# Two products of the identity with itself ahead of each block's and each chain chunk's own products

## The chip, the cores and the metric

The kernel runs on one core of a Trainium2 chip. The metric is the device time of one execution in microseconds (us). Five engines matter here: PE (TensorE, matrix products; PEld are its weight loads), DVE (VectorE), ACT (ScalarE), POOL (GpSimd), and SP, which issues most transfers. TensorE's clock has two levels, 2.4 GHz and 1.2 GHz; the profile shows the granted one as 1.00 and 0.50.

## The reference

Two layers of a network over 512 latent and 256 context positions of width 1024. Each layer is a feed-forward part, a token mixing and a second feed-forward part. The mixing projects the input once, runs a windowed attention over four pairs of heads, and on the other half of the width a recurrence in both directions of time:

```python
px = nx @ w_in
attn_x = neighbourhood_attention(q_x, k_x, v_x, k_s, v_s, na_bias)
def step(S, inp):                       # 8 heads, two directions
    removal = jnp.einsum('bhvk,bhk->bhv', S, kk_t)
    S = S * w_t - removal[..., None] * (kk_t * a_t) + v_t[..., None] * k_t
    out = jnp.einsum('bhvk,bhk->bhv', S, r_t)
...
y_x = jnp.concatenate([attn_x, rwkv_x], axis=-1) @ w_out
```

Layer 0 also carries the context stream through the mixing's output; layer 1 does not.

## The kernel before

Activations lie with the width on the 128 partitions and the 768 positions along the free axis. The feed-forward parts stream weights and multiply in split float32. The change sits in the token mixing, `mix`.

`mix` runs several generators side by side through `drive` (line 74): `chains` (rank 0), `solves` (rank 1), `all_blocks` (rank 2), and, all at rank 3, `projections`, the modulation products of the coming parts (`fillers`), `attentions` and `outs` (the output projection). `drive` steps them by a model time; each step's instructions get a priority from the rank, and the framework's scheduler then orders every engine's instructions by readiness and priority. So the order on PE is not written out by hand: it is one in-order queue that the scheduler fills from all streams.

The recurrence is computed in chunks of 32 positions, in two groups of two head pairs, 24 chunks a group:

- `rwkv_block` (line 811) prepares, for one pair `p` and one half `u` of 128 positions, the operands (DVE, POOL and ACT), and at line 884 takes a PSUM bank `gt` from the tag `p` for each of the two directions and runs eight products of 64 rows by 64 columns into it (line 887). ACT and DVE copy the result into the stage tile `st`. There are 24 blocks and 48 such banks in a layer. `free_stage` holds back all but the first four blocks of a layer until `qkv_done[NP - 1]`, that is, until the projections are done.
- `rwkv_solve` and `rwkv_solves` invert the chunk's triangular systems: DVE work, then small products into `py`, `px` (lines 928, 936) and `ap` (line 790). These banks are also of the tag `p`, which has two banks in all; `lz` (line 828) and `bops` (line 745) use it too.
- `rwkv_chain` (line 945) carries the state from chunk to chunk. Line 969 takes the bank `ch`; the tag `ch` has one bank. Eight products (line 972) read the state `x`, ACT and DVE copy half of the bank back into `x`, eight products (line 978) fill the other half, and ACT and DVE copy that into `x2`, the next chunk's `x`. There are 48 chunks in a layer.

A product of float32 operands is two MATMUL instructions with a weight load each. `self.c(C_ID)` is a 128 by 128 identity that lies in SBUF from the start.

Of the kernel before, what the change touches and what calls it, by code (L numbers as in the profile page):

```python
# [29 lines left out]
H, HD, NP = 8, 64, 4  # L30
# [5 lines left out]
C_ID, C_MEAN, C_B64, C_J, C_MG, C_RST, C_BO2, C_EPS = (  # L36
    0, 128, 130, 258, 386, 450, 706, 708)
# [12 lines left out]
def rev(ap):  # L50
    a = [list(x) for x in ap.ap]
    s, n = a[-1]
    return bass.AP(tensor=ap.tensor, offset=ap.offset + s * (n - 1), ap=a[:-1] + [[-s, n]])


def free_ap(ap, dims, offset=0):
    return bass.AP(tensor=ap.tensor, offset=ap.offset + offset, ap=[list(ap.ap[0])] + [list(d) for d in dims])
# [52 lines left out]
class Net:  # L110
# [700 lines left out]
    def rwkv_block(self, l, p, b, emit, ltd, g):  # L811

        nc = self.nc
        y = p % 2
        ts = g["ts"][y]
        ins = [g["in"][y, n] for n in (b, (0, 2, 1)[b])]
        r, k, kk = [[t[:, n] for t in ins] for n in range(3)]
        lora = self.wp.tile([128, 2, 128], F32, name="lora", bufs=2)
        nc.sync.dma_start(out=lora, in_=self.a["lora"][l, :, :, 128 * p:128 * p + 128])
        spans = [self.span(b, d) for d in range(2)]  # L820
        order = lambda t, d: rev(t) if d else t

        th, tan = self.t("sp", "th", 512), self.t("sp", "tan", 512)
        for i, t in enumerate((th, tan)):
            rows = HALVES[i]
            ps = self.bank("p", "lz", (128, 2, 256))
            for d in range(2):
                nc.tensor.matmul(ps[:, d], lhsT=lora[rows, d], rhs=self.zin[rows, spans[d]], start=True, stop=True)
            for d in range(2):
                n = 8 * i + 4 * d + p  # L830
                self.act(t[:, 256 * d:256 * d + 256], order(ps[:, d], d), AF.Tanh, scale=0.5 - i, bias=self.rv[:, n:n + 1])
        if b == 0:
            self.tt(ts[:, spans[0]], tan[:, 0:256], rev(tan[:, 256:512]), ALU.add)
        else:
            for d in range(2):
                src = order(tan[:, 256 * d:256 * d + 256], d)
                if b == 1:
                    nc.gpsimd.tensor_scalar(ts[:, spans[d]], src, 1.0, None, ALU.mult)
                else:
                    self.tt(ts[:, spans[d]], ts[:, spans[d]], src, ALU.add)  # L840
        nc.vector.tensor_scalar(th, th, 1.0, None, ALU.add)
        for d in range(2):
            cs = slice(256 * d, 256 * d + 256)
            nc.vector.tensor_tensor_scan(out=th[:, cs], data0=self.c(C_RST, 256), data1=th[:, cs], initial=0.0, op0=ALU.mult, op1=ALU.add)
        pd = self.t("sp", "pd", 520).rearrange("p (s t) -> p s t", t=65)
        nc.gpsimd.memset(pd[:, :, 0:1], 1.0)
        self.act(pd[:, :, 1:65], th.rearrange("p (s t) -> p s t", t=64), AF.Exp, scale=-0.5 * DC)
        self.act(th, th, AF.Exp, scale=0.5 * DC, bias=self.eps(1))
        bks = []
        for d in range(2):  # L850
            kd, kkd = order(k[d], d), order(kk[d], d)
            c8 = lambda t: t.rearrange("p (c t) -> p c t", c=8)
            bk = self.t("sp", "bk", 512).rearrange("p (c a t) -> p c a t", c=8, a=2)
            ka, be = bk[:, :, 0], bk[:, :, 1]
            td = c8(tan[:, 256 * d:256 * d + 256])
            self.stt(be, td, -1.0, c8(kkd), ALU.add, ALU.mult)
            nc.gpsimd.tensor_scalar(ka, td, self.rv[:, 24 + p:25 + p], self.rv[:, 16 + p:17 + p], ALU.mult, ALU.add)
            self.tt(ka, ka, c8(kd), ALU.mult)
            self.tt(bk, bk, free_ap(th[:, 256 * d:256 * d + 1], [[32, 8], [0, 2], [1, 32]]), ALU.mult)
            bks.append(bk)  # L860
        for h in range(2):
            u = 2 * b + h
            yield from self.until(lambda: self.free_stage(p, u))
            st = self.t("st", "st", SW)
            g["stage"][y, u] = st
            c4 = lambda t: t.rearrange("p (s h t) -> p s h t", s=2, h=2)
            for e, rows in enumerate(SR):

                o = 1024 * e
                one = self.consts[rows, C_ID + 64 * e:C_ID + 64 * e + 64]  # L870
                nc.vector.tensor_scalar(free_ap(st[rows], [[256, 4], [1, 64]], o), free_ap(one, [[0, 4], [1, 64]]), 1.0, None, ALU.mult)
                self.tt(free_ap(st[rows], [[512, 2], [256, 2], [1, 64]], o + 128), free_ap(one, [[0, 2], [0, 2], [1, 64]]),
                        free_ap(pd[rows, 2 * h:2 * h + 1, 64], [[260, 2], [65, 2], [0, 64]]), ALU.mult, nc.gpsimd)
                if not emit:
                    nc.gpsimd.memset(free_ap(st[rows], [[128, 8], [1, 32]], o + 64), 0.0)
                for d in range(2):
                    now = slice(128 * (h ^ d), 128 * (h ^ d) + 128)
                    pq = pd[rows, 4 * d + 2 * h:4 * d + 2 * h + 2]
                    bl = self.blocks(st, e, d)[rows].rearrange("p (s h) m -> p s h m", h=2)
                    self.tt(bl[:, :, :, B_U], c4(order(kk[d][rows, now], d)), pq[:, :, 0:64].rearrange("p s (h t) -> p s h t", h=2), ALU.mult, self.nc.gpsimd)  # L880
                    if emit:
                        self.tt(bl[:, :, :, B_O], c4(order(r[d][rows, now], d)), pq[:, :, 1:65].rearrange("p s (h t) -> p s h t", h=2), ALU.mult)
            for d in range(2):
                gt = self.bank("p", "gt", (128, 4, 128))
                for c in range(4):
                    for e, rows in enumerate(SR):
                        nc.tensor.matmul(gt[SR[1 - e], c], lhsT=bks[d][rows, 4 * h + c].rearrange("p a t -> p (a t)"),  # L887
                                         rhs=self.block(st, e, d, c)[rows], start=True, stop=True)
                for e, rows in enumerate(SR):
                    o = SR[1 - e]  # L890
                    bl = self.blocks(st, e, d)
                    self.act(bl[o, :, B_S], gt[o, :, B_S], AF.Copy)
                    self.tt(bl[o, :, 64:128], gt[o, :, 64:128], free_ap(self.c(C_MG)[o], [[0, 4], [1, 64]]), ALU.mult)
                    n = 16 * y + 8 * d + 4 * h
                    nc.vector.tensor_scalar(ltd[UR[e], n:n + 4], bl[UR[e], :, B_U], 1.0, None, ALU.mult)
            yield E["b"]

    def free_stage(self, p, u):

# [45 lines left out]
    def rwkv_chain(self, l, i, last):  # L945
# [8 lines left out]
        for u in range(6):  # L954
# [9 lines left out]
            for c in range(4):  # L964
                j = 4 * u + c
                if j < 23:
                    self.rwkv_values(i, j + 1)
                x, x2 = self.xs[j % 4], self.xs[(j + 1) % 4]
                ps = self.bank("ch", "ch", (128, 2, 4, 64))
                for y, d, n in heads:  # L970
                    for e, k in enumerate((slice(0, 96), slice(0, 128))):
                        nc.tensor.matmul(ps[UR[e], 0, n], lhsT=bl(y, e, d, c)[k, B_U], rhs=x[k, e, n], start=True, stop=True)  # L972
                self.act(x[UR[0], 0], ps[UR[0], 0], AF.Copy)
                nc.vector.tensor_copy(x[UR[1], 1], ps[UR[1], 0])
                if j < 23:
                    for y, d, n in heads:
                        for e, rows in enumerate(SR):
                            nc.tensor.matmul(ps[rows, 1, n], lhsT=bl(y, e, d, c)[:, B_S], rhs=x[:, e, n], start=True, stop=True)  # L978
                    self.act(x2[SR[0], 0], ps[SR[0], 1], AF.Copy)
                    nc.vector.tensor_copy(x2[SR[1], 1], ps[SR[1], 1])  # L980
                if emit:
                    for y, d, n in heads:
                        for e in range(2):
                            nc.tensor.matmul(po[QUADS[c], e, n], lhsT=bl(y, e, d, c)[:, B_O], rhs=x[:, e, n], start=True, stop=True)  # L984
                yield E["c"]
# [334 lines left out]
```

## Time and profile before

| | |
|---|---|
| median of 3 runs | 3880.44 us (3858.85 to 3891.40) |
| the profiled execution's own time | 3867.65 us |
| its span, first to last instruction | 3865.8 us |
| PE busy | 3593.8 us (93%), 28980 MATMULs |
| PE weight loads | 3116.1 us (81%) |
| DVE busy | 2918.1 us (75%) |
| ACT busy | 1503.8 us (39%) |
| POOL busy | 1078.3 us (28%) |
| granted TensorE clock, mean | 0.938 |

A MATMUL's end is modelled and neighbours overlap, so a busy PE is not a PE at its peak. The page's slices divide the span into 40 parts of 96.6 us; a digit is tenths. The chain of waits is followed back from the last instruction and here reaches back to about 2790 us, so it covers layer 1's mixing but not layer 0's.

### The profile page before, as it was taken

The page shows a single profiled execution, that of the slowest core. Times are in us where ns is not written, and L with a number is a line of the kernel's source. Part 1 is how long each engine was busy: PE and PEld are TensorE (multiplying, and loading weights), DVE is VectorE, ACT ScalarE, POOL GpSimd, SP SyncE. Part 2 cuts the span into 40 slices and gives each one's busy share as a digit, 9 for nine tenths or more (in the row PEclk, how much of TensorE's full clock was granted, in tenths as well). Part 3 has the DMA queues.
Part 4 walks back from the last instruction along what each step waited for, and adds up shares of the span by engine and source line. Part 5 has one row for each costly group of instructions (what it writes and reads, how often), then busy time and mean ns, then how long its engine had stood idle before and what let it go on. Part 6 is the DMA issues. An engine that isn't in the chain of part 4 may idle for free. (4 is left out here: it accounts for less than half of the span.)

```text
span 3865.8 us, 73287 instructions
## 1 busy us (share of the span) xinstructions
PE 3593.8 (93%) x28980; PEld 3116.1 (81%) x28980; DVE 2918.1 (75%) x5612; ACT 1503.8 (39%) x2996; POOL 1078.3 (28%) x1208
## 2 busy tenths in 40 slices
PE   6999999999899899899998999999999996879999
PEld 4789998787665667799998999998786665768999
DVE  6578786666777776888888888886668677667878
ACT  5233334334343433433335333334434343244433
POOL 3222230202222211322233222230203123124665
PEclk9999999999798799899998999999999895789999
DMA  5321113322345263112211111213333431221232
GB/s 205 122 86 66 69 63 101 99 92 79 98 139 160 74 194 96 36 66 72 76 69 47 66 66 66 76 63 113 105 101 121 147 97 33 76 66 66 88 108 79
DMA packets 213943, 352.50 MB, mean 91 GB/s; under 512 B 46432, under 2 KB 128992, under 8 KB 201312
## 3 DMA queue, kind: packets, MB, share of 16 engines
q1 hardware_dynamic: 213600, 347.81, 27.7%
q8 instruction: 229, 3.75, 0.4%
q14 instruction: 114, 0.93, 0.1%
HBM read 305.26 MB, written 42.47 MB: 90 GB/s over the span
## 5 line engine op out<-in xcount | busy, mean ns | idle before, releaser
L394 PE MATMUL mw<-b,wq 128*128 128x386 f32 (+1 forms) x4224 | 788.6, 329 | 18.4 <-DVE wq L165 13.3
L394 PEld LDWEIGHTS mw<-b,wq 128*128 128x128 f32 x4224 | 705.0, 191 | 38.8 <-DVE wq L165 17.7
L352 PE MATMUL mm<-h,whi 128*128 128x256 f32 (+1 forms) x2816 | 650.1, 326 | 2.8 <-ACT h L171 1.8
L394 PE MATMUL mw<-b,whi 128*128 128x386 f32 (+1 forms) x2112 | 518.6, 328 | 14.9 <-DVE b L165 8.3
L168 DVE SCALAR_TENSOR_TENSOR x<-mm,mods,x 128x256 f32<-128x256 f32 (+1 forms) x704 | 390.7, 581 | 184.8 <-PE mm L352 181.3
L352 PEld LDWEIGHTS mm<-h,whi 128*128 128x128 f32 x2816 | 465.8, 188 | 58.4 <-issue 8.9
L352 PE MATMUL mm<-h,wlo 128*128 128x256 f32 (+1 forms) x1408 | 439.8, 325 | 2.0 <-DVE wlo L165 1.9
L394 PEld LDWEIGHTS mw<-b,whi 128*128 128x128 f32 x2112 | 374.3, 191 | 20.6 <-DVE b L165 10.5
L171 ACT ACTIVATE whi<-wraw 128x512 fp32r<-128x512 f32 x312 | 195.9, 629 | 490.1 <-PE mm L352 274.2
L165 DVE TENSOR_TENSOR wq<-raw,wq 128x512 fp32r<-128x512 f32 x352 | 312.8, 891 | 55.7 <-ACT wq L171 53.4
L394 PE MATMUL mw<-b,wlo 128*128 128x386 f32 (+1 forms) x1056 | 347.0, 329 | 3.6 <-DVE wlo L165 2.7
L171 ACT ACTIVATE wq<-raw 128x512 fp32r<-128x512 f32 x352 | 220.1, 629 | 303.7 <-PE mw L394 284.7
L352 PEld LDWEIGHTS mm<-h,wlo 128*128 128x128 f32 x1408 | 261.6, 188 | 27.9 <-DVE wlo L165 2.6
L165 DVE TENSOR_TENSOR up_g<-up_g,mw 128x386 f32<-128x386 f32 (+1 forms) x352 | 181.9, 517 | 78.8 <-PE mw L394 69.1
L165 POOL TENSOR_TENSOR raw<-raw,s 128x512 f32<-128x512 f32 x88 | 122.0, 1386 | 400.3 <-DVE wq L165 396.5
L165 DVE TENSOR_TENSOR wlo<-wraw,whi 128x512 fp32r<-128x512 f32 x268 | 186.3, 696 | 51.5 <-ACT whi L171 34.9
L171 ACT ACTIVATE whi<-s 128x512 fp32r<-128x512 f32 x176 | 110.1, 628 | 281.5 <-PE mm L352 199.2
L165 POOL TENSOR_TENSOR s<-raw 128x512 f32<-128x512 f32 x88 | 127.6, 1450 | 304.7 <-DVE wlo L165 293.9
L352 PE MATMUL mm<-x,whi 128*128 128x258 f32 (+2 forms) x832 | 209.2, 337 | 0.1
L394 PEld LDWEIGHTS mw<-b,wlo 128*128 128x128 f32 x1056 | 201.4, 191 | 7.6 <-DVE wlo L165 7.1
L165 POOL TENSOR_TENSOR up_g<-up_g,rstd 128x386 f32<-128x386 f32 (+1 forms) x88 | 107.0, 1216 | 346.6 <-DVE up_g L165 346.6
L188 PE MATMUL modps<-wmod,cs 128*32 128x256 f32 x1152 | 164.8, 443 | 28.1 <-DMA wmod<-in_w_mod_dram 27.3
(249 smaller groups left out, 7090.9 us busy)
## 6 DMA issues: line engine op xcount, KB each, us to landing
raw<-in_ffn_up_dram SPq DMA_DIRECT2D x88, 1024.0 KB, 5.2
wmod<-in_w_mod_dram SPq DMA_DIRECT2D x208, 256.0 KB, 3.0
wraw<-in_ffn_down_dram SPq DMA_DIRECT2D x176, 256.0 KB, 3.1
wraw<-in_w_in_dram SPq DMA_DIRECT2D x104, 256.0 KB, 2.9
wmod<-in_w_mod_dram SPq DMA_DIRECT2D x96, 128.0 KB, 2.3
wmod<-in_w_mod_dram SPq DMA_DIRECT2D x8, 1024.0 KB, 10.8
wraw<-in_w_out_dram SPq DMA_DIRECT2D x32, 256.0 KB, 3.1
in<-rkv SPq DMA_DIRECT2D x20, 384.0 KB, 3.7
```

What stands on the lines that cost most here:

```text
L165: (eng or self.nc.vector).tensor_tensor(out=out, in0=a, in1=b, op=op)
L168: self.nc.vector.scalar_tensor_tensor(out=out, in0=a, scalar=s, in1=b, op0=op0, op1=op1)
L171: self.nc.scalar.activation(out, in_, f, **kw)
L188: nc.tensor.matmul(ps[q:q + 32], lhsT=self.cs[:, kt], rhs=w, start=kt == 0, stop=kt == KD - 1)
L352: nc.tensor.matmul(ps, lhsT=wt, rhs=xt[k][:, c0:c1], start=k == 0 and n == 0, stop=k == nk - 1 and n == 2)
L394: nc.tensor.matmul(ps, lhsT=wt[:, c], rhs=self.bs[i][k][xt], start=k == 0 and m == 0, stop=k == 3 and m == 2)
```

## The change

A new method, `fill`, writes the product of the identity with itself into the given columns, 128 at a time, once the layer's projections have all been issued. It is called on the first 256 columns of each `gt` bank and on the second half (256 columns) of each `ch` bank, ahead of the bank's own products, which overwrite what it wrote. Nothing reads it.

```diff
             for d in range(2):
                 gt = self.bank("p", "gt", (128, 4, 128))
+                self.fill(gt.rearrange("p c t -> p (c t)")[:, 0:256])
                 for c in range(4):
...
+    def fill(self, ps):
+
+        if self.qkv_done[NP - 1]:
+            for c in range(0, ps.shape[1], 128):
+                self.nc.tensor.matmul(ps[:, c:c + 128], lhsT=self.c(C_ID), rhs=self.c(C_ID), start=True, stop=True)
...
                 ps = self.bank("ch", "ch", (128, 2, 4, 64))
+                self.fill(ps[:, 1].rearrange("p n t -> p (n t)"))
                 for y, d, n in heads:
```

## Rows read from the trace of the kernel before

**Rows 1.** The page: busy times, slices of PE and its clock, chain by engine.
```profile
PE 3593.8 (93%) x28980; PEld 3116.1 (81%) x28980; DVE 2918.1 (75%) x5612; ACT 1503.8 (39%) x2996; POOL 1078.3 (28%) x1208
...
PE   6999999999899899899998999999999996879999
...
PEclk9999999999798799899998999999999895789999
...
PE 16%; DVE 8%; issue 1%; ACT 1%; DMA 1%; POOL 0%; SPq 0%; ACTq 0%; POOLq 0%; DVEq 0%
```

**Rows 2.** Stretches of both mixings after their projections: busy us, count, clock, DMA.
```profile
core 0: us, PE busy (x) PEld busy (x) DVE busy (x) ACT busy (x) POOL busy (x), PEclk, DMA share, GB/s
985.00:1510.00 525.00, 476.26 (x5994) 334.15 (x5994) 376.95 (x888) 212.88 (x504) 118.10 (x210) 0.87 0.43 134
2960.00:3430.00 470.00, 406.89 (x5369) 308.00 (x5370) 344.80 (x797) 178.50 (x422) 104.43 (x185) 0.82 0.31 95
```

**Rows 3.** The chain of waits from 2960 to 3430 us, share by line.
```profile
by line: PE ap L790 7.7%; PE mm L352 7.0%; DVE st L165 5.3%; PE gt L887 5.2%; PE co L984 4.6%; issue 4.4%; PE ch L972 4.0%; DVE pr L165 3.9%; PE modps L188 3.9%; PE ch L978 3.8%; PE px L936 3.4%; PE py L928 3.2%; PE pv L629 2.9%; DVE k L918
```

**Rows 4.** Tiles vtps and ch, by window: count, ns min/median/max, first and last start.
```profile
L538 PE MATMUL vtps<-consts,v x24: 270/272/329, 760.6 to 996.0; 128*128 128x128 f32 x24
...
L538 PE MATMUL vtps<-consts,v x48: 270/272/329, 760.6 to 2961.9; 128*128 128x128 f32 x48
...
L972 PE MATMUL ch<-k,st x638: 217/219/317, 1025.9 to 1501.9; 96*32 96x64 f32 x122, 128*32 128x64 f32 x38
...
L972 PE MATMUL ch<-k,st x638: 217/219/317, 3001.5 to 3426.7; 96*32 96x64 f32 x143, 128*32 128x64 f32 x17
```

**Rows 5.** Pieces of the chain: start us, us, what. Same work, both clock levels.
```profile
2909.63 1.55 PE hrb L496 x12
3023.25 1.89 PE gt L887 x32
3100.23 1.44 PE ap L790 x32
3206.95 0.85 PE pg L1073 x4
3217.38 0.85 PE pg L1073 x4
3219.73 1.22 PE pj L1051 x2
3229.29 0.45 PE pg L1073 x4
3320.07 3.68 PE gt L887 x32
3372.92 2.70 PE ap L790 x32
```

**Rows 6.** Stretches of 5 us in layer 1's mixing, columns as in rows 2.
```profile
3215.00:3220.00 5.00, 4.45 (x96) 3.86 (x93) 1.33 (x3) 1.75 (x4) 1.78 (x3) 0.50 0.21 54
3220.00:3225.00 5.00, 4.83 (x44) 3.60 (x46) 2.92 (x7) 1.38 (x3) 1.32 (x3) 0.50 0.09 28
...
3250.00:3255.00 5.00, 1.43 (x22) 1.19 (x24) 4.57 (x11) 0.38 (x1) 0.80 (x1) 0.50 0.11 33
3265.00:3270.00 5.00, 0.07 (x2) 0.08 (x4) 4.72 (x11) 1.51 (x4) 0.00 (x0) 0.50 0.00 0
...
3290.00:3295.00 5.00, 5.00 (x68) 4.50 (x64) 3.15 (x8) 1.83 (x4) 0.00 (x0) 0.50 0.06 13
3295.00:3300.00 5.00, 5.00 (x60) 3.93 (x58) 1.59 (x4) 1.56 (x4) 0.00 (x0) 0.50 0.01 5
```

**Rows 7.** Tiles pd and ap: a clearing ahead of its tile, and a bank's copies.
```profile
L846 POOL MEMSET pd<- x2: 112/114/117, 3240.2 to 3277.7; 128x8 f32 x2
L171 ACT ACTIVATE pd<-th x2: 628/629/630, 3243.3 to 3311.7; 128x512 f32<-128x512 f32 x2
...
L171 ACT ACTIVATE st<-ap x40: 467/482/485, 3017.5 to 3392.4; 32x384 f32<-32x384 f32 x40
L795 DVE COPY st<-ap x40: 540/550/551, 3018.1 to 3392.9; 32x384 f32<-32x384 f32 x40
```

## The prediction, made before the changed kernel ran

> **What bounds the kernel now.** I read the page first. PE is busy for 93% of the span and has most of the chain that ended last, 16% of the span against 8% for DVE and 1% each for issue, ACT and DMA; the chain covers only the last quarter [rows 1]. The clock digits are 9 almost everywhere, but sag to 7, 8 and 5 in two places, the two token mixings, where the change is [rows 1]. So I cut those out: from the end of the projections to the last chain chunk is 985 to 1510 us in layer 0 and 2960 to 3430 us in layer 1. PE is busy for 476 of 525 us and 407 of 470 us, at a mean clock of 0.87 and 0.82 [rows 2]. With levels of 1.00 and 0.50 that is (1 - 0.87) x 2 x 525 = 137 us and (1 - 0.82) x 2 x 470 = 169 us at the half level, 306 us in all, 31% of these 995 us.
>
> Who sets the end there? In layer 1 the PE lines that the chain lists add up to 46% of the stretch, and the list is cut off [rows 3]; over the whole chain PE has 16 of 27 parts, 59% [rows 1]. I take 55%. The reader is to see a mixed bound: a little over half of the path is PE's in-order queue, the rest mostly DVE preparing operands. Layer 0 lies outside the chain; its PE is busy for 91% against layer 1's 87%, so I use the same 55%.
>
> **The change, part by part.** Nothing is removed or moved; no transfer, DVE, ACT or POOL instruction is added.
>
> How many. `free_stage` keeps all blocks but four of a layer's 24 behind the projections, so 20 blocks x 2 directions = 40 `gt` banks a layer are filled. Chunks 0 to 7 need only those first four blocks; the other 40 chunks a layer come behind. The trace agrees: the last projection products run at 996 and 2962 us, and behind these 638 MATMULs of line 972, at 16 a chunk, are 40 chunks in each layer [rows 4]. So 160 fills, 320 products, 640 MATMULs and 640 weight loads; the page's counts should go from 28980 to 29620.
>
> What one costs. The kernel has the same work already: `pg` is two float32 products of 128 by 128 by 128, four MATMULs. As a piece of the chain it took 0.85 us at the half level and 0.45 us where the clock came up [rows 5]. The twelve-instruction `hrb` gives 1.55 x 4 / 12 = 0.52 us at the full level [rows 5]. I take 0.48 and 0.85, and with the present 31% at the half level 0.69 x 0.48 + 0.31 x 0.85 = 0.59 us. All 160 together: 95 us of PE time.
>
> What of it is on the path. Ahead of a chunk, the fill cannot hide in the chunk's own wait: there is one `ch` bank, it comes free when ACT and DVE have copied the state out of it, and these copies are what the chunk's products wait for as well. So each of these fills lengthens the chain's step by its whole time, where the chain or the PE queue is the path. Ahead of a block the fill needs only a bank, while the block's products need operands from DVE and POOL; there it hides whenever PE waits for those. The bounds are nothing (all in PE's idle time: 49 us in layer 0 and 63 us in layer 1 [rows 2], enough room for it) and 95 us (all on the path). I take PE's share of the path, 0.55 x 95 = 52 us: 160 fills are spread over the same work that the share was read from.
>
> What it can give back. The same work at the two levels: 32 `gt` MATMULs 3.68 and 1.89 us, 32 of `ap` 2.70 and 1.44 us [rows 5], a saving of 47 to 49%; I take 45%, since waits between pieces do not shrink. Of the 306 us at the half level 55% is PE on the path, 168 us, so the clock fully restored would be worth 0.45 x 168 = 76 us. That is the upper bound, and nothing the lower.
>
> How much of it comes? The rows speak for little. From 3290 to 3300 us PE was busy for 10.00 of 10 us and the level stayed 0.50 [rows 6]. From 3217 to 3221 us the queue ran `pg` and `pj`, full-height products like the fill, for 0.85 and 1.22 us, and the level stayed 0.50 up to 3225 us [rows 5, 6]: more than one fill's worth, without effect. The other half-level stretches are DVE's: at 3250 and 3265 us PE was busy for 1.43 and 0.07 of 5 us [rows 6], and a fill stands ahead of a chunk or a block, which such a stretch has few of. One fill every 6.2 us (160 in 995 us) is thin. I take a fifth, 15 us.
>
> The Trainium skill ("TensorE: Matmul & The Clock Gate", Part 1) says that the default state is throttled and that activity releases the throttle. Taken at its word, the fills would release it throughout, and the sum would be the faster rival's below; the rows at 3217 and 3290 us disagree in part.
>
> The same page (Part 3) has a rule against the change: a weight load overlaps running products only where its row group differs, and the fill's takes all rows. By it each fill would show one weight load more; `pg`'s 0.45 us holds its loads already, so the row adds nothing.
>
> The sum: 3867.65 + 52 - 15 = 3905 us on the profiled execution's own time, +1.0%. That execution was 12.8 us below the median of the runs shown, whose spread is 32.5 us, so an after of 3905 to 3918 us would be the same result; I predict 3910, +0.8% on the median.
>
> **The rivals.** (1) Faster: the fills hold the clock up. For it: every sag of the clock lies where the fills go, and they are full-height work. Against it: rows 6. All 160 fills then cost 0.48 x 160 x 0.55 = 42 us and 76 come back: 3834 us; with the block fills hidden in waits, 21 instead of 42, it is 3813 us. It decides from about two thirds of the half-level time gone.
>
> (2) Slower, the banks of tag `p` are held: a block's fill waits for no operand, so the scheduler can issue it as soon as a `p` bank is free, and the bank then stays taken until the block's operands are there. It does so elsewhere: the clearing of `pd` ran at 3277.7 us, its filling at 3311.7, 34 us later [rows 7]. With one of two banks held, `ap` products cannot run while the bank before is copied out, 0.48 + 0.55 = 1.03 us each [rows 7]. A layer has 48 such banks; if a third of the 96 meet it, that is 33 us on top: 3867.65 + 52 + 33 - 15 = 3938 us. It decides from some twenty such banks. Against it: the solves have a higher priority than the blocks and their products take the bank first when both are ready.
>
> (3) Slower by more of the path: DVE's waits give no cover, PE's share is 0.8 rather than 0.55, and the clock does not move: 3867.65 + 76 = 3944 us; the end of this is all 95 us, 3963.
>
> (4) The change does nothing to the time: the scheduler puts the fills into PE's idle stretches, which the 112 us of rows 2 can hold, and the clock gives back the rest: 3855 to 3875 us. For it: fills are ready early. Against it: the chunk fills, half of them, are not.
>
> **How the numbers follow.** A measurement of this kernel can tell about 1% from no change, 39 us on 3880. My forecast (3885 to 3919 us) has a chance of 0.35, rival 4 of 0.13; together within 1%, 0.48. Rivals 2 and 3 have 0.20 and 0.18, slower by over 1%, 0.38. Rival 1 has 0.14, faster by over 1%. The range leaves out the far part of rival 1 and the end of rival 3: 3845 to 3950 us, with the unknown costs (0 to 95 on the path, 0 to 76 back) inside it as far as they are likely together. The forecast's own range is 3885 to 3919.
>
> **What would show it.** MATMULs 29620 on the page; the fill's line at 0.45 to 0.85 us for four instructions. The mean clock over the two mixings: a fifth of the half-level time gone would be 0.90 and 0.86; above 0.95 in both is rival 1, unchanged is rival 3. In the chain of waits the fill's line should show in layer 1 with some 26 us, chunk fills most of it. Rival 2 shows as idle PE ahead of `ap`, `py` or `lz` ended by ACT or DVE copies, and as a long time between a block's fill and its products. I am wrong if the span moves by more than the fills and the clock together account for, which would mean that the scheduler's new order, not the work added, made the difference.

## The result, and the profile after

The median went from 3880.44 to 3907.25 us (3893.09 to 3913.82, 7 runs): a ratio of 1.0077, with an interval of 1.0054 to 1.0100. That is inside the range, 2.75 us from the predicted time. It is within the 1% that the prediction gives as what a measurement can tell from no change, but seven runs of each kernel put the interval above 1: the kernel is a little slower. The profiled execution took 3904.54 us, against the sum's 3905; its span is 3902.7 us.

The page after, to be held against [rows 1]: busy time, the slices of PE and of its clock, the chain by engine.

```profile
PE 3664.0 (94%) x29620; PEld 3177.7 (81%) x29620; DVE 2909.4 (75%) x5612; ACT 1501.0 (38%) x2994; POOL 1075.9 (28%) x1208
...
PE   6999999999899898899999999999998997989999
...
PEclk8999999999899898899999999999998896789999
...
PE 17%; DVE 7%; issue 1%; POOL 1%; ACT 1%; DMA 0%; SPq 0%; ACTq 0%; POOLq 0%; DVEq 0%
```

The count is 29620, as worked out. The two sags of the clock digits are shallower than in [rows 1] (7, 9, 8, 7 became 8, 9, 9, 8 in layer 0, and the lowest digit of layer 1 went from 5 to 6), but they are still there. The two stretches of [rows 2], in the kernel after:

```profile
core 0: us, PE busy (x) PEld busy (x) DVE busy (x) ACT busy (x) POOL busy (x), PEclk, DMA share, GB/s
985.00:1510.00 525.00, 489.47 (x6219) 349.09 (x6219) 364.57 (x867) 207.94 (x490) 115.36 (x205) 0.93 0.42 131
2960.00:3430.00 470.00, 426.15 (x5320) 321.14 (x5319) 338.93 (x796) 170.99 (x405) 109.19 (x197) 0.84 0.29 94
```

The clock rose from 0.87 to 0.93 and from 0.82 to 0.84. At levels of 1.00 and 0.50 that leaves 74 + 150 = 224 of the 306 us at the half level: 82 us are gone, 27%, where the prediction took a fifth. The fills themselves, line 903 over the whole kernel (count: ns min/median/max of one MATMUL, first and last start, forms):

```profile
L903 PE MATMUL gt<-consts x320: 270/275/582, 908.0 to 3370.4; 128*128 128x128 f32 x160
...
L903 PE MATMUL ch<-consts x320: 270/275/583, 933.4 to 3464.1; 128*128 128x128 f32 x160
...
its engine sat idle before it (us, times) until:
  DVE k L988: 36.9, 22
```

Line 988 is the copy that frees the `ch` bank: a chunk's fill waits for it, as its products did before. (The first fills run some 90 us ahead of the last projection product: they are emitted behind the projections, but are ready earlier.) In the chain of waits of layer 1's mixing, 2989 to 3468 us, the rows that answer [rows 3]:

```profile
by line: PE ap L790 7.8%; PE mm L352 5.3%; PE modps L188 4.9%; PE co L992 4.9%; PE gt L888 4.9%; DVE st L165 4.4%; PE ch L986 4.2%; DVE pr L165 4.0%; PE ch L980 3.8%; PE pv L629 3.7%; PE ch L903 3.7%; issue 3.7%; PE px L943 3.3%; PE py L935
```

The chunk fills have 3.7% of 479 us, 18 us, on the chain, where the prediction put some 26 us for all fills; block fills do not reach the list, which is cut off. By this view alone block fills would be free and chunk fills the whole price. The experiments show that this is not so.

Last, what the scheduler did with a block's fill. PE's timeline of the kernel after (start us, us, what):

```profile
3085.50 0.71 PE L903 MATMUL gt<-consts 128*128 128x128 f32 x4
...
3088.32 0.71 PE L903 MATMUL gt<-consts 128*128 128x128 f32 x4
...
3092.93 0.71 PE L903 MATMUL ch<-consts 128*128 128x128 f32 x4
3093.57 0.47 PE L980 MATMUL ch<-k,st 96*32 96x64 f32 x10
...
3102.71 1.52 PE L888 MATMUL gt<-st,bk 64*64 64x128 f32 x23
```

Two `gt` banks are filled at 3085.5 and 3088.3 us, and their own products come at 3102.7 us. In between PE runs attention, modulation and chain products. Taken over all 80 block fills (from the start of the fill's last MATMUL to the first of its own products, banks taken in order), 37 have more than 1 us between the two, 34 more than 5 us, the longest 30.4 us. A chunk's fill always stands directly ahead of its products, as at 3092.9 us.

These rows also give the price of one fill in PE's queue, from its first MATMUL to the start of the next product. At 3092.93 us, at the full level, that is 0.64 us, and it is the median of all fills that ran at this level. At the half level it is 1.15 us:

```profile
3284.81 1.22 PE L903 MATMUL ch<-consts 128*128 128x128 f32 x4 [1.50 <-DVE k L988]
3285.96 1.07 PE L980 MATMUL ch<-k,st 96*32 96x64 f32 x16
```

The prediction took 0.48 and 0.85 us.

### The profile page after: what moved, and what is told of

Read it like the earlier page. It is cut to its first block, busy times and chain, and to the rows that moved or that the text cites. A ratio compares the mean times of both kernels' runs of the same rounds, so it can differ in the third digit from the quotient of the medians.

```text
span 3902.7 us, 74575 instructions
## 1 busy us (share of the span) xinstructions
PE 3664.0 (94%) x29620; PEld 3177.7 (81%) x29620; DVE 2909.4 (75%) x5612; ACT 1501.0 (38%) x2994; POOL 1075.9 (28%) x1208
## 5 line engine op out<-in xcount | busy, mean ns | idle before, releaser
L394 PEld LDWEIGHTS mw<-b,whi 128*128 128x128 f32 x2112 | 373.4, 190 | 17.6 <-DVE b L165 10.4
L165 DVE TENSOR_TENSOR wlo<-wraw,whi 128x512 fp32r<-128x512 f32 x268 | 187.2, 699 | 55.4 <-ACT whi L171 35.5
```

What stands on the lines that cost most here:

```text
L165: (eng or self.nc.vector).tensor_tensor(out=out, in0=a, in1=b, op=op)
L394: nc.tensor.matmul(ps, lhsT=wt[:, c], rhs=self.bs[i][k][xt], start=k == 0 and m == 0, stop=k == 3 and m == 2)
```

## The experiments

In all of them the fills' results are overwritten and never read, so nothing of the computation is left out. Two kinds of edit are used. One is made in the source, and the scheduler then finds **an order of its own**, which differs from others all over the mixing. The other is made behind the scheduler, on the finished instruction list, so that **one order** (that of the kernel after, or of the kernel before) is kept on every engine.

**Which fills?** One of the two calls is taken out; each kernel has an order of its own.

```diff
 # e1_gt_only
-                self.fill(ps[:, 1].rearrange("p n t -> p (n t)"))
 # e2_ch_only
-                self.fill(gt.rearrange("p c t -> p (c t)")[:, 0:256])
```

> The fills ahead of the blocks alone, 80 of 160. Theory A (the fills' PE time on the path, less what the clock gives back): somewhat under half of the whole change's +27 us, since blocks wait for DVE operands and part of these fills hides, +5 to +13 us. Theory B (a fill takes a bank of tag p early and holds it, and the scheduler's new order costs): most of the loss is here, +20 to +30 us.

> The fills ahead of the chain's chunks alone, 80 of 160. Theory A: these cannot hide in the chunk's own wait, so over half of the loss, +14 to +25 us. Theory B: no second bank is held and little is reordered, 0 to +7 us.

Block fills alone: 3877.35 us, ratio 1.0000 (0.9978 to 1.0023), which neither theory had. Chunk fills alone: 3898.03 us, 1.0048 (1.0025 to 1.0071), some 19 us, as theory A had it. So 80 block fills cost nothing in sum, with a mean clock over the runs of 0.946 against 0.932 for the kernel before; that is not yet to say that they are hidden.

**Do the rows of the array matter?** The fill is computed from 32 of the 128 rows, or cut to one product of 32 by 32 by 16. Orders of their own again.

```diff
 # e3_rows32
-                self.nc.tensor.matmul(ps[:, c:c + 128], lhsT=self.c(C_ID), rhs=self.c(C_ID), start=True, stop=True)
+                self.nc.tensor.matmul(ps[:, c:c + 128], lhsT=self.c(C_ID)[0:32], rhs=self.c(C_ID)[0:32], start=True, stop=True)
 # e4_thin
-            for c in range(0, ps.shape[1], 128):
-                self.nc.tensor.matmul(ps[:, c:c + 128], lhsT=self.c(C_ID), rhs=self.c(C_ID), start=True, stop=True)
+            self.nc.tensor.matmul(ps[0:32, 0:16], lhsT=self.c(C_ID)[0:32, 0:32], rhs=self.c(C_ID)[0:32, 0:16], start=True, stop=True)
```

> Both kinds of fill with the identity's first 32 rows only: as many instructions, columns and banks, about the same PE time, but a quarter of the array's rows at work. Theory A: the same cost and less or none of the clock relief, which I put at 15 us by the prediction and at 30 us by the traces' fall in half-level time: +42 to +57 us against before, mean clock in the two mixings back near 0.87 and 0.82. Theory B: no difference from the whole change, +27 us.

> One product of 32 by 32 by 16 per fill instead of two of 128 by 128 by 128: the same places, banks and guard, but about 0.05 us of PE time (py's piece of 108 MATMULs took 1.81 us). Theory A: 160 x 0.05 = 8 us of PE, about half on the path, no clock relief: 0 to +8 us. Theory B: as much as the whole change, +20 to +35 us, since the bank is taken as early and the order is disturbed as much.

With 32 rows: 3975.77 us, 1.0259 (1.0213 to 1.0305). Cut small: 3903.69 us, 1.0063 (1.0039 to 1.0088). Products of the same columns on a quarter of the rows cost 1.8% more than those on all rows, and the mean clock of the runs is 0.930; +100 us is far more than either theory had. The small products came out at +24 us, inside theory B's 20 to 35. But each order is another one, so the next two repeat it in the order of the kernel after.

```diff
 # behind the scheduler, on the instruction list
+    _refit(nc, 32, 32, 16)        # e5: each of the 320 products becomes 32 rows, 32 weights, 16 columns
+    _refit(nc, 32, 128, 128)      # e6: 32 rows, weights and columns as they were
```

> The changed kernel in its own order on every engine; only once that order stands is each fill's product cut down from 128 by 128 by 128 to 32 by 32 by 16. So the order and the banks' early taking stay, the fills' time goes, and so does what they do for the clock. Theory A (the loss is the fills' own time on the path, less what the clock gives back): 0 to +8 us against before. Theory B (the loss is the new order and the banks taken early): as much as the changed kernel or more, +20 to +50 us.

> The changed kernel in its own order, each fill's product with 32 of the 128 rows: same instructions and columns. Against the changed kernel it tells what the full height gives back through the clock, with nothing else changed. If that is a fifth of the half-level time, as I predicted: +15 us over the changed kernel, +42 against before. If it is most of it (theory C): +50 to +75 us over the changed kernel, +80 to +100 against before.

Small: 3897.33 us, 1.0049 (1.0025 to 1.0074), 19 us, above theory A and at the lower edge of B. With 32 rows: 3939.07 us, 1.0187 (1.0148 to 1.0227), where full height gives 1.0077. The fill's line in the 32-row kernel:

```profile
L903 PE MATMUL gt<-consts x320: 270/270/577, 908.0 to 3397.4; 32*128 32x128 f32 x160
```

One MATMUL of 32 rows takes 270 ns where one of 128 rows takes 275. In the queue a fill of 32 rows takes 0.64 us at the full level, as one of full height does. The work is the same and the time is 1.1% longer: the difference, about 43 us, is what full height gives back, between the 15 us of a fifth and the 50 us or more of "most". A small fill takes 0.22 us in the queue (median at the full level), not the 0.05 us that its expectation worked with.

**The order of before.** The 160 fills are put into the list of the kernel before, each in front of its bank's first product, whose wait it takes over. So no bank is taken early and no other instruction moves.

```diff
 # behind the scheduler, in the order of the kernel before
+    _insert(nc, ("gt", "ch"))         # e7: 128 rows
+    _insert(nc, ("gt", "ch"), 32)     # e8: 32 rows
+    _insert(nc, ("gt",))              # e11: block fills alone, 128 rows
```

> The kernel before in its own order, with the same 160 fills put in front of the same banks after that order stood; each fill takes over the wait of the bank's first product, so none is issued early and none hides in that wait. Theory A: +27 us or more, up to the +52 of the path share less the clock's part. Theory B: clearly less than the changed kernel, -10 to +10 us.

> As the run before, with 32 of 128 rows in each fill's product. Its distance to that run is what the full height gives back through the clock in the old order: 15 us for a fifth, 50 to 75 us for most of it.

> The order of the kernel before, with the 80 block fills alone put in front of the banks' first products, behind the waits of these. With both kinds of fill so placed it stood at 1.0156, +60 us. Theory 'place': a block's fill is cheap only where it runs ahead of its products' wait; put behind it, it costs as a chunk fill does, so half of the 60 us, +25 to +35, 1.006 to 1.009. Rival 'kind': block fills are cheap wherever they stand, because the path seldom runs through the blocks, so +0 to +10, 1.000 to 1.0025, and the chunk fills cost 50.

All fills: 3932.62 us, 1.0156 (1.0123 to 1.0190). With 32 rows: 3958.82 us, 1.0230 (1.0191 to 1.0269). Block fills alone: 3913.64 us, 1.0077 (1.0049 to 1.0104). All fills are 60 us, above theory A's 52, and full height gives back some 29 us here. Behind their products' waits block fills cost 30 us of the 60: theory "place" had 1.006 to 1.009 for it. That chunk fills cost the other 30 is a subtraction; they were not run alone in this order.

**What is the order of the kernel after worth by itself?** The fills are taken out of its finished list, and the next product takes over their waits; the same for the kernel with block fills alone.

```diff
 # behind the scheduler, in the order of the kernel after, and of e1
+    _drop(nc)      # all fills go; a fill's waits are carried by the next product in PE's queue
```

> The order of the changed kernel on every engine, with all 160 fills taken out; a wait that a fill carried is carried by the next product in TensorE's queue. Nothing of the computation is left out. Before this run the same order with fills of 32 by 32 by 16 stood at 1.0049 of the kernel before, +19 us. Theory 'order': the scheduler's new order, with banks taken early and waits moved forward, is what costs, so without any fill the kernel stays at 1.003 to 1.006, +12 to +23 us. Rival 'instructions': the small fills themselves cost the 19 us (640 more products and weight loads), so without them the time is that of the kernel before, 0.998 to 1.002. In between, each has its part.

> The order of the kernel with block fills alone, with its 80 fills taken out in the same way. With the fills it stood at 1.0000. Theory 'order': taking the p banks early has a price of its own here too, some +10 us or 1.003, which the clock gave back. Rival: this order costs nothing, 0.999 to 1.001, so work and clock of the block fills cancel by themselves. A third: the order is better than before's by chance, 0.997 or less, and the block fills cost what it gains.

Order of after, no fill: 3865.80 us, 0.9964 (0.9943 to 0.9986). Order of e1, no fill: 3879.51 us, 0.9999 (0.9975 to 1.0023). Theory "order" is out: the order with its early-taken banks and the waits moved forward is in sum no slower than that of before. "Instructions" was right in kind: the 19 us of the small fills, and more, are the price of 640 small MATMULs and their weight loads (160 x 0.22 = 36 us of queue). So e4 and e5 came near theory B's numbers for another reason than B's. The result of e9 on the fast side was expected by neither; e10 came out as its rival had it. e9 is also the fastest kernel of all these, though by 0.36% only.

**More of the free kind.**

```diff
 # e12, block fills alone, an order of its own
-                self.fill(gt.rearrange("p c t -> p (c t)")[:, 0:256])
+                self.fill(gt.rearrange("p c t -> p (c t)"))
```

> Block fills alone, over the whole bank: four products of the identity instead of two, in an order of its own. With two it stood at 1.0000. Theory 'work and clock cancel': twice the fill gives twice the work and less than twice the relief, since half of the half-level time in layer 0 was gone already: 1.002 to 1.006. Rival 'hidden work, more clock': the fills run in TensorE's waits and cost nothing, so more of them gives a higher clock and a faster kernel: 0.994 to 0.998, with the mean clock of the two mixings above 0.91 and 0.86.

3920.06 us, 1.0102 (1.0073 to 1.0131): worse than either theory had it. Here twice the fill added work and gave no more clock, but in an order that is another one too, so the two kernels differ in more than the fills. The mixings of e1, block fills, from 985 to 1530 and from 2960 to 3500 us (columns as in the windows above):

```profile
985.00:1530.00 545.00, 499.09 (x6190) 352.74 (x6188) 383.98 (x914) 218.78 (x516) 125.47 (x221) 0.91 0.42 130
2960.00:3500.00 540.00, 452.64 (x5704) 347.62 (x5700) 391.94 (x891) 209.20 (x499) 128.27 (x215) 0.84 0.29 89
```

The same stretches of e12, block fills doubled:

```profile
985.00:1530.00 545.00, 505.93 (x6268) 362.63 (x6266) 375.49 (x891) 215.15 (x505) 120.68 (x212) 0.90 0.42 131
2960.00:3500.00 540.00, 475.52 (x5828) 367.20 (x5829) 375.13 (x875) 197.05 (x459) 123.81 (x214) 0.84 0.30 91
```

The same of e10, the order of e1 with its fills taken out:

```profile
985.00:1530.00 545.00, 492.79 (x5990) 343.46 (x5988) 369.86 (x879) 212.14 (x499) 118.08 (x209) 0.85 0.42 129
2960.00:3500.00 540.00, 452.14 (x5630) 345.04 (x5628) 404.45 (x920) 212.13 (x502) 138.66 (x231) 0.81 0.30 93
```

In these profiled executions block fills lift the clock from 0.85 and 0.81 to 0.91 and 0.84; doubled, they leave it at 0.90 and 0.84.

**Work and clock taken apart, in all runs.** Every run comes with its span and its mean granted clock, so each gives the time at the half level: 2 x (1 - clock) x span. Among the runs of one kernel the instructions are the same, yet the spans differ, and they go with that time. Over 180 runs of the kernels here (each kernel's runs against their own mean) a microsecond more at the half level goes with 0.37 us more of span (standard error 0.01, correlation 0.94). What is left of the spread has a standard deviation of 3.5 us, where it was 10.4. So most of the spread goes with the clock. With this price each kernel's distance from the kernel before (mean span 3875.3 us, 518 us at the half level, the mean of three groups, 67 runs in all, whose means lie 6 us apart) splits into a clock part and a rest, the rest being what it would be at the same half-level time:

| kernel | runs | mean span | at the half level | span against before | clock part | rest |
|---|---|---|---|---|---|---|
| after | 7 | 3903.7 | 414 | +28.4 | -38.1 | +66.5 |
| e9, order of after, no fill | 12 | 3865.0 | 497 | -10.3 | -7.4 | -2.9 |
| e5, order of after, small | 12 | 3892.9 | 511 | +17.5 | -2.6 | +20.1 |
| e6, order of after, 32 rows | 6 | 3945.6 | 535 | +70.2 | +6.5 | +63.7 |
| e1, block fills | 12 | 3879.3 | 423 | +4.0 | -34.8 | +38.7 |
| e10, order of e1, no fill | 12 | 3877.8 | 501 | +2.5 | -6.1 | +8.6 |
| e12, block fills doubled | 6 | 3920.2 | 460 | +44.9 | -21.1 | +66.0 |
| e2, chunk fills | 12 | 3895.8 | 477 | +20.4 | -15.0 | +35.5 |
| e11, order of before, block fills | 6 | 3910.6 | 481 | +35.3 | -13.4 | +48.7 |
| e7, order of before, all fills | 6 | 3933.5 | 458 | +58.1 | -22.0 | +80.1 |
| e8, the same, 32 rows | 6 | 3961.8 | 536 | +86.5 | +6.8 | +79.7 |
| e3, own order, 32 rows | 6 | 3977.4 | 560 | +102.1 | +15.4 | +86.7 |
| e4, own order, one small product | 10 | 3902.3 | 524 | +26.9 | +2.3 | +24.7 |

The split holds where it can be tried: full height and 32 rows, in one order, have the same rest (66.5 and 63.7 us; 80.1 and 79.7 us) and differ in the clock part alone. These pairs give the price a second time, from an edit: 41.9 us of span for 121 us at the half level and 28.3 us for 78 us, 0.35 and 0.36. The 0.37 itself rests on how runs vary together; no run here sets the clock by itself. Two orders without fills have rests of -2.9 and +8.6 us, so kernels with orders of their own (e1 to e4, e12) carry some 10 us that is not the fills'.

The windows show the clock of single executions. The kernel after itself stands at 0.93 and 0.84 in these stretches; e9, its order without fills:

```profile
985.00:1530.00 545.00, 498.52 (x5952) 349.05 (x5951) 366.05 (x873) 210.08 (x495) 115.17 (x205) 0.82 0.41 126
2960.00:3500.00 540.00, 458.83 (x5691) 352.16 (x5687) 402.85 (x928) 212.00 (x500) 130.59 (x228) 0.82 0.30 93
```

And e6, its order with fills of 32 rows:

```profile
985.00:1530.00 545.00, 515.71 (x6241) 367.25 (x6240) 365.67 (x870) 209.37 (x492) 115.28 (x205) 0.88 0.41 127
2960.00:3500.00 540.00, 503.14 (x5944) 386.62 (x5940) 377.48 (x882) 191.90 (x449) 119.17 (x216) 0.83 0.28 88
```

The same of e7, the order of before with fills of 128 rows, and of e8, with 32:

```profile
985.00:1530.00 545.00, 502.07 (x6179) 354.40 (x6178) 369.78 (x869) 207.31 (x491) 116.53 (x208) 0.91 0.42 128
2960.00:3500.00 540.00, 477.63 (x5937) 366.18 (x5935) 381.94 (x889) 197.61 (x459) 126.07 (x222) 0.87 0.29 89
985.00:1530.00 545.00, 508.15 (x6139) 358.29 (x6138) 365.72 (x862) 206.00 (x487) 115.46 (x206) 0.87 0.41 127
2960.00:3500.00 540.00, 487.01 (x5520) 367.78 (x5519) 358.00 (x831) 182.62 (x423) 118.23 (x209) 0.78 0.27 84
```

The profiled execution of e9 was that kernel's slowest, 3888.0 us of span against a mean of 3865.0, so its 0.82 in layer 0 is low for it. The 32-row fills are PE work too (503 us of 540 busy in e6), and with them the clock is lower than with full height: 0.87 and 0.78 against 0.91 and 0.87 in the order of before; in that of after 0.88 against 0.93 in layer 0, but 0.83 against 0.84 in layer 1. For that order the difference rests on the means over runs in the table, 535 against 414 us.

## Why the prediction came out right, and which of its terms did not

The sign, the size and the mechanism were right: the fills lengthen PE's queue, the clock gives a part back, and the difference is a slowdown of under 1%. But both terms were too small, and their errors cancelled; that the result lies within 3 us of the forecast is luck.

- **How many**: right. 640 MATMULs, 160 of each kind in a layer, at a median of 275 ns each, as a product of this size takes elsewhere (272 ns in [rows 4]).
- **What one costs**: too small. A fill takes 0.64 us in the queue at the full level and 1.15 us at the half level, not 0.48 and 0.85. The pieces in [rows 5] are stretches of a chain of waits, shorter than the time in the queue, and the products chosen stood next to others of 128 by 128. In the kernel before, the same four MATMULs of `pg` take 0.64 us between products of other shapes and 0.36 us between products of 128 by 128 (start us, us, what; clock 1.00 in both):

```profile
1268.69 0.71 PE L1073 MATMUL pg<-sg,gg 128*128 128x128 f32 x4
1269.33 0.45 PE L978 MATMUL ch<-k,st 128*64 128x64 f32 x8
...
3415.34 0.61 PE L1073 MATMUL pg<-sg,read 128*128 128x128 f32 x4
3415.70 0.49 PE L352 MATMUL mm<-o,whi 128*128 128x256 f32 x2
```

  The `pg` of 3217.18 us, read as 0.85 us, is followed by the next product after 0.99 us. A fill mostly stands between products of other shapes (64 by 128 ahead of it and 96 by 32 behind it at 3092.93 us), so it pays the higher price. Its 0.64 us is 0.19 more than the 0.45 us read from `pg`, about one weight load (192 ns); so the ground on which the prediction set a further weight load aside does not hold, though no run shows that it is the weight load that takes the time.
- **What is on the path**: too small. The 52 us were 0.55 x 95. At equal half-level time the fills cost 66.5 + 2.9 = 69 us in the order of after and 80 us in the order of before. At that time what is added runs at the full level, 160 x 0.64 = 103 us of queue (an estimate from the median), so 0.67 and 0.78 of it went into the span. The 32-row fills of e6 give 0.65 (67 of 102 us) and the small fills of e5 0.64 (23 of 36 us). So the share was higher than 0.55, in the order of after by about a fifth; the price of one fill was off by more, a third. With 0.64 and 1.15 the prediction's own working would have had 0.69 x 0.64 + 0.31 x 1.15 = 0.80 us a fill, 128 us in all, 70 us of it on the path; e6 against e9, span against span with no half-level time held equal, is 81 us.
- **What comes back**: too small. In the two stretches of the profiled executions 82 us of the 306 went, where a fifth is 61; they were predicted at a clock of 0.90 and 0.86 and came out at 0.93 and 0.84. Over the whole span and in the mean of all runs it is 104 us (518 to 414). Each was worth 0.37 us instead of 0.55 x 0.45 = 0.25. At 0.37, the 104 us are 38 us instead of 15; e6 against after, in medians, gives 43. The second factor has the same share in it: 0.37 / 0.45 is 0.82.
- **Where block fills hide**: in part. The step said that they hide in waits for DVE and POOL, and chunk fills do not. At equal clock 80 block fills (51 us of queue) cost 38.7 - 8.6 = 30 us in the order found for them; if that held in the order of after, chunk fills would have about 39 of its 69. Behind the waits it is 49 us for block fills and, by subtraction, 31 us for chunk fills. Differences of 10 us here are at the edge of what such runs tell. What makes block fills free in sum is the clock: 423 us at the half level with them, 501 in the same order without.
- **Rows 6 as evidence**: right that fills would not hold the clock up throughout, wrong to take PE's busy time there as activity of the fill's kind. PE's timeline of the kernel before (start us, us, what) shows what kept it busy:

```profile
3288.72 2.77 PE L790 MATMUL ap<-st,tt 32*32 32x96 f32 x32
3291.42 1.12 PE L978 MATMUL ch<-k,st 128*64 128x64 f32 x16
3292.47 2.77 PE L790 MATMUL ap<-st,tt 32*32 32x96 f32 x32
3295.18 1.07 PE L972 MATMUL ch<-k,st 96*32 96x64 f32 x16
3296.17 2.12 PE L790 MATMUL ap<-st,tt 32*32 32x96 f32 x22
```

  Most of it is `ap`, products over 32 rows by 32 columns of the array: a part of its rows, as in e6 and e8, whose fills brought no clock. That this is why the level stayed low there is inferred from those two, not tried by itself.
- **The sum**: 52 - 15 = +37 us; measured 69 - 38 - 3 = +28 us, the last 3 being the order. The cost was 17 us short and the relief 23 us. The share stood in both terms, so its error cancels in part by construction; that the price of a fill and the fall in half-level time were both too small did so by chance. In e6, with 32 rows, the clock part is +6 and the span +70: with no relief to cancel it, the cost term of 52 us would have been 18 us short.

The rivals. (1) Faster: its mechanism is real, but 82 of the 306 us went, where two thirds were named as the point from which it decides. (2) Banks held: the early fills came, 34 of them more than 5 us ahead of their products, more than the twenty from which it was to decide, and no cost is seen: the order made with them is at 0.9964 without its fills. (3) More of the path on PE: its share of 0.8 is nearer than 0.55 to the 0.78 of the order of before, and 0.67 in the order of after lies halfway; it was wrong in leaving the clock where it was. (4) No change: out, since PE's idle time took too little of the work. What was to show the scheduler's order as the cause, a span that fills and clock do not account for, is not seen: the rest of e9 is -2.9 us.

The Trainium skill ("TensorE: Matmul & The Clock Gate", Part 1) says that activity releases the throttle, and the trace agrees for full-height products: 83 us less at the half level in one order (497 to 414). For products on 32 rows it does not: 535 us against those 497, with PE busy for 94% of the span against 93%. The same page of the Trainium skill ("Why this matters for your kernels") says that a single product over 32 rows takes as long as one over 128; 270 and 275 ns agree.

What stays open: why the same four MATMULs take longer between products of other shapes, and why 0.78 of the added queue time reached the end in the order of before and 0.65 to 0.67 in that of after. By the page after, PE has 17 of the chain's 27 parts, 0.63, and DVE 7. Open too is why block fills that run early bring more clock (78 us of half-level time, e10 to e1) than the same fills behind the waits (37 us, e11 against before).

## What to carry to other kernels

Where one in-order engine is busy for over 90% of a stretch, count most of the work added to its queue as time (here 0.64 to 0.78 of it). Price that work by the time from its first instruction to the next one's start, next to the neighbours that it will have: by a piece of the chain it came out a quarter too cheap. Price work and clock separately; the run-to-run spread of one kernel gives an estimate of the clock's price without any edit, to be held against a pair of runs in one order that differ in the clock alone. Useless full-height products do lift TensorE's clock, but here at a price above what they give back, so they gained at best nothing (block fills, 1.0000).

## What of the hardware was not expected

- Four MATMULs of 128 by 128 by 128 take 0.64 us in the queue between products of other shapes, 0.36 us between products of 128 by 128, both at the full level.
- Products on 32 rows of the array take as long as those on 128 (270 and 275 ns) and cost the kernel as much at equal half-level time, but bring no higher clock: 535 and 536 us at the half level, against 414 and 458 with full height in the same orders.
- The spread between runs of one kernel goes mostly with its clock: correlation 0.94 over 180 runs, 0.37 us for a microsecond at the half level. The profiled execution of before, 12.8 us below its median, had a mean clock of 0.938 where that kernel's runs have 0.933.
- More filling did not bring more clock: 423 us at the half level with two products a block, 460 us with four, in two different orders.
